# The second feed-forward block's input product: seven half-size products in place of eight from the third tile on

## The chip, the cores and the metric

One core of one Trainium2 chip runs the kernel. The metric is the device time of one execution in microseconds; the time of a version is the median of its runs.

## What is computed

One block of a diffusion transformer, depth 1, on 512 tokens and 256 context tokens of width 1024: a feed-forward block, a mixer (window attention and a gated linear recurrence), and a second feed-forward block. The change concerns the second feed-forward block, which is, for the 512 tokens:

```python
def swiglu(h, w_in, w_out):
    gate, up = jnp.split(h @ w_in, 2, axis=-1)
    return (jax.nn.silu(gate) * up) @ w_out

h = ada_pre(x, norm_pre[l, 2], m[6], m[7])        # rmsnorm, scale, shift
x = ada_post(x, swiglu(h, ffn2_w_in[l], ffn2_w_out[l]), norm_post[l, 2], m[8], 0.5)
```

`w_in` is 1024 x 5632 (gate columns first, then up columns), `w_out` is 2816 x 1024, all in float32.

## The kernel before

Every float32 matrix product runs as three matmuls on operands that were split into a high part (rounded to the engine's short float32 form) and a low residue: `split` makes them with a cast on ScalarE (L65) and a subtraction on VectorE (L66), and `mm3` issues high x high, high x low and low x high (L71, L72, L74) into one PSUM accumulation.

The second feed-forward block keeps the hidden activations transposed, as high and low tiles "hh" and "hl" of 128 partitions x 8 k x tokens. `make_hT` makes them two 128-token groups at a time: for each k two transposes into PSUM (L248), scale and shift (L253 or L255), a cast and a subtraction on VectorE (L257, L258). Its second half is for tokens 256 to 511, which come last from the output projection of the mixer (`y_step`).

`ffn` then walks over 22 tiles, each one 128-column piece of the gate and the same piece of the up weights. For a tile, `in_w` loads a weight piece of 1024 x 128 ("wraw", 512 KB, three buffers) and splits it into "wh" and "wl" (three buffers each); `proj` multiplies it by all 512 tokens: 8 k x 3 matmuls of 512 columns for the gate and the same for up. Then a Silu on ScalarE (L333), the product on VectorE (L335) and a split give "acth" and "actl". The first three weight pieces (both of tile 0, the gate of tile 1) are loaded and split early (`pre2`) and are multiplied in two groups of 256 tokens (`proj_all`), so that TensorE can begin on the first tokens while the last ones are still being made.

Tiles are taken in pieces of 1, 3, 3, 3, 3, 3, 2, 4 (`PIECES`). After the first tile of a piece, `out_phase` multiplies the previous piece's activations by their output weights (`out_w`, buffer "w4" for the raw load, "woh" and "wol" split): for each of four token groups two 512-column halves, added to "yacc" or "tok" (L363, L365). In time, therefore, three input tiles alternate with the output stretch of three tiles.

`mod_gate(2, ...)` makes the gate vector of the last norm from 4 MB of `w_ada`: 16 loads ("wa", two buffers), 16 multiply-adds on VectorE into "macc" (L496, L498), two pairs of matmuls with ones (L507, L508). It stands in the list `background`, and `tick` issues from that list; at the block's first tick all of it is issued, since credit is left over from the first feed-forward block.

The order on each engine's queue is not written by hand here: the framework places instructions by program order as priority, by when it reckons that operands and buffers are ready. All loads are issued on SyncE's queue (SP). [...]

## Time and profile before

| | |
|---|---|
| median of 3 runs | 1497.29 us (1496.05 to 1497.7) |
| the profiled execution | 1498.88 us, its span 1497.1 us |
| mean granted clock of TensorE | 0.991 of full speed |
| busy share of the span | TensorE 97%, VectorE 58%, ScalarE 34% |
| second feed-forward block | from about 1119 us to the end |

Times in rows are microseconds from the span's start. "PE" is TensorE's matmuls, "PEld" its weight loads, "DVE" VectorE, "ACT" ScalarE, "POOL" GpSimd, "SP" the load queue. A duration in a row may overlap the next instruction's, so the distance from one start to the next is the time that an instruction takes of a busy engine.

### The profile page before, as it was taken

What the parts mean: (1) busy time and instruction counts of PE and PEld (TensorE: products, weight loads), DVE (VectorE), ACT (ScalarE), POOL (GpSimd) and SP (SyncE); (2) the same over time, 40 slices, a digit from 0 to 9 for tenths busy, and PEclk for the clock granted to TensorE, in tenths of its full rate; (3) what the DMA queues carried; (4) which work ended last, traced back from release to release, by engine and by line L of the source; (5) the groups of instructions that cost most, each with busy time, mean ns of one, the idle gap of its engine ahead of it and who ended that gap; (6) DMA issues with size and microseconds to landing.
All of it is one profiled execution on the core that took longest, in us unless ns stands there. A gap on an engine that the chain in (4) does not pass through costs nothing.

```text
span 1497.1 us, 20626 instructions
## 1 busy us (share of the span) xinstructions
PE 1445.2 (97%) x8320; PEld 1204.6 (80%) x8320; DVE 870.3 (58%) x1431; ACT 515.9 (34%) x835; POOL 58.3 (4%) x87
## 2 busy tenths in 40 slices
PE   6899999999999999999999899999999999999997
PEld 3688888888788888788889777788778788888886
DVE  6866664675655333857488579843457544433444
ACT  6532121222121222543234468742246222222221
POOL 3200000000000000200001100000010000000001
PEclk9999999999999999999999989999999999999999
DMA  8564332454542111222112211133226533333301
GB/s 305 174 198 128 113 113 69 119 165 141 175 149 71 57 33 53 86 76 61 30 58 60 61 56 43 29 99 99 99 85 207 173 99 99 91 93 106 94 26 56
DMA packets 177895, 151.45 MB, mean 101 GB/s; under 512 B 6408, under 2 KB 152328, under 8 KB 177800
## 3 DMA queue, kind: packets, MB, share of 16 engines
q1 hardware_dynamic: 177800, 150.14, 32.8%
q8 instruction: 65, 1.06, 0.3%
q14 instruction: 30, 0.25, 0.0%
HBM read 148.02 MB, written 2.10 MB: 100 GB/s over the span
## 4 chain that ended last, share of the span: by engine, by line
PE 71%; issue 15%; DVE 6%; ACT 3%; DMA 2%; POOL 2%; SPq 0%; DVEq 0%; POOLq 0%; ACTq 0%
PE mm L71 22%; PE mm L72 22%; PE mm L74 22%; DMA wa<-w_ada 1%; POOL rs L227 1%; PE aux L929 1%; DVE wl L66 1%; DVE wa0l L178 1%; ACT w L224 1%; POOL ss L226 1%; ACT wh L65 0%; PE aux L935 0%; PE aux L507 0%; PE aux L936 0%; DMA tok<-ctx 0%
## 5 line engine op out<-in xcount | busy, mean ns | idle before, releaser
L71 PE MATMUL mm<-hh,wh 128*128 128x512 f32 (+1 forms) x1440 | 513.0, 356 | 0.5 <-ACT sg L333 0.2
L72 PE MATMUL mm<-hl,wh 128*128 128x512 f32 (+1 forms) x1440 | 491.8, 355 | 0.0
L74 PE MATMUL mm<-hh,wl 128*128 128x512 f32 (+1 forms) x1440 | 449.0, 357 | 0.3 <-DVE wl L66 0.3
L71 PEld LDWEIGHTS mm<-hh,wh 128*128 128x128 f32 x1440 | 271.3, 188 | 58.7 <-ACT gg L794 0.7
L72 PEld LDWEIGHTS mm<-hl,wh 128*128 128x128 f32 x1440 | 271.3, 188 | 39.8 <-DVE hl L426 0.6
L65 ACT CAST wh<-wraw 128x1024 fp32r<-128x1024 f32 (+1 forms) x139 | 142.4, 1026 | 461.1 <-PE mm L72 299.9
L66 DVE TENSOR_TENSOR wl<-wraw,wh 128x1024 fp32r<-128x1024 f32 (+1 forms) x139 | 165.5, 1192 | 222.1 <-ACT wh L65 218.9
L74 PEld LDWEIGHTS mm<-hh,wl 128*128 128x128 f32 x1440 | 244.3, 189 | 21.3 <-DVE wl L66 0.5
L71 PE MATMUL mm<-woh,acth 128*128 128x512 f32 x420 | 164.5, 392 | 2.4 <-DVE am L335 2.2
L72 PE MATMUL mm<-wol,acth 128*128 128x512 f32 x420 | 164.1, 391 | 0.0
L498 DVE SCALAR_TENSOR_TENSOR macc<-wa,cs,macc 128x512 f32<-128x512 f32 x140 | 101.8, 750 | 63.3 <-DMA wa<-w_ada 62.6
L74 PE MATMUL mm<-woh,actl 128*128 128x512 f32 x420 | 130.7, 390 | 0.0
L335 DVE TENSOR_TENSOR am<-sg,mm 128x512 f32<-128x512 f32 x66 | 37.5, 595 | 116.0 <-PE mm L74 115.9
L65 ACT CAST woh<-w 128x1024 fp32r<-128x1024 f32 x42 | 44.3, 1055 | 167.9 <-PE mm L74 163.7
L71 PEld LDWEIGHTS mm<-woh,acth 128*128 128x128 f32 x420 | 78.8, 188 | 20.9 <-DVE am L335 3.1
L74 PEld LDWEIGHTS mm<-woh,actl 128*128 128x128 f32 x420 | 78.8, 188 | 16.6
L72 PEld LDWEIGHTS mm<-wol,acth 128*128 128x128 f32 x420 | 78.9, 188 | 15.8
L365 DVE TENSOR_TENSOR tok<-tok,mm 128x512 f32<-128x512 f32 x96 | 61.6, 683 | 51.6 <-PE mm L74 51.6
L66 DVE TENSOR_TENSOR wol<-w,woh 128x1024 fp32r<-128x1024 f32 x42 | 51.2, 1223 | 15.7 <-ACT woh L65 14.4
L226 POOL TENSOR_SCALAR ss<-ss 128x1 f32<-128x1 f32 x30 | 10.4, 345 | 973.2 <-ACT am L224 550.0
L65 ACT CAST acth<-am 128x512 fp32r<-128x512 f32 x66 | 34.1, 549 | 23.4 <-DVE am L335 23.2
L66 DVE TENSOR_TENSOR actl<-am,acth 128x512 fp32r<-128x512 f32 x66 | 37.5, 597 | 0.7 <-ACT acth L65 0.7
(286 smaller groups left out, 1698.6 us busy)
## 6 DMA issues: line engine op xcount, KB each, us to landing
wraw<-ffn_w_in SPq DMA_DIRECT2D x88, 512.0 KB, 4.1
wa<-w_ada SPq DMA_DIRECT2D x128, 256.0 KB, 3.1
w<-ffn_w_out SPq DMA_DIRECT2D x44, 512.0 KB, 4.3
wraw<-mix_w_in SPq DMA_DIRECT2D x42, 512.0 KB, 3.7
tok<-w_ada SPq DMA_DIRECT2D x16, 256.0 KB, 5.6
wraw<-w_out SPq DMA_DIRECT2D x8, 512.0 KB, 4.2
tok<-x SPq DMA_DIRECT2D x4, 512.0 KB, 7.8
wraw<-x SPq DMA_DIRECT2D x4, 512.0 KB, 3.2
```

Source lines behind the costliest of these rows:

```text
L65: nc.scalar.copy(hi, src)
L66: nc.vector.tensor_tensor(out=lo, in0=src, in1=f32(hi), op=ALU.subtract)
L71: nc.tensor.matmul(o, lhsT=sh, rhs=mh, start=start, stop=False)
L72: nc.tensor.matmul(o, lhsT=sh, rhs=ml, start=False, stop=False)
L74: nc.tensor.matmul(o, lhsT=sl, rhs=mh, start=False, stop=stop)
L178: eng.tensor_tensor(out=wl, in0=w, in1=f32(wh), op=ALU.subtract)
L224: nc.scalar.activation(scratch, z, AF.Square, accum_out=ss)
L226: nc.gpsimd.tensor_scalar(ss, ss, 1.0 / n, EPS, ALU.mult, ALU.add)
L227: nc.gpsimd.tensor_tensor(out=r, in0=ss, in1=mhalf, op=ALU.pow)
L335: nc.vector.tensor_tensor(out=m[:, :b - a], in0=s[:, :b - a], in1=up, op=ALU.mult)
L365: nc.vector.tensor_tensor(out=y, in0=y, in1=o[h], op=ALU.add)
L498: nc.vector.scalar_tensor_tensor(out=a, in0=w, scalar=cs[:, v, k:k + 1], in1=a, op0=ALU.mult, op1=ALU.add)
```

## The change

The 2 x 2 x 2 block product (gate and up weights; lower and upper half of k; first and second 256 tokens) is done with seven block products in place of eight, by Winograd's form of Strassen's method, for tiles 2 to 21. Each block product is 4 k x 3 matmuls of 256 columns (`product`). The sums of weight blocks are made for every tile by four VectorE additions of 128x512 (`weights`), with three 1024-wide splits and a 512-wide one in place of two 1024-wide ones. Block sums of the activations (four of them, `sums2`, `sums2_t4`) are made once and kept split beside the blocks themselves, seven forms in all, in the tiles "hh" and "hl". The seven products run through three PSUM accumulators A, B and C; intermediate values are read out of A and C by copies on ScalarE and additions on VectorE before later products are added on top of them. Tiles 0 and 1 are done in the ordinary way, in halves of 256 tokens (`std_tile`).

Around it: `hT_forms` replaces `make_hT` (the cast of two chunks at a time on ScalarE); "w4" moves to a pool of its own ("bx") and holds the unsplit activation blocks too, until the sums are made; `mod_gate` enters the background list after tile 1; the attention's "ov" has one buffer instead of two; the second two token groups are normalised in place; `out_w` and `out_phase` move unchanged into `run_pieces`.

```diff
--- before.py
+++ after.py
@@ -305,7 +305,6 @@
 
         gmax = max(b - a for a, b in groups)
         early = []
-        order = order or range(ntok)
 
         def in_w(j, u):
             return split_w(load_w(w_in[:, u * FF + j * P:u * FF + (j + 1) * P]))
@@ -336,8 +335,13 @@
                 split(ah[:, a:b], al[:, a:b], m[:, :b - a])
             return ah, al
 
+        run_pieces(in_tile, w_out, ntok, pool, pieces, yacc, last, final_pre, order)
+    def run_pieces(in_tile, w_out, ntok, pool, pieces, yacc, last, final_pre=None, order=None, w4=None):
+        order = order or range(ntok)
         def out_w(j):
-            raw = ct([P, D], "w4", bufs=3 if ntok == NX else 4, pool=pool)
+            raw = ct([P, D], "w4", bufs=4, pool=w4 or pool)
             nc.sync.dma_start(raw, w_out[j * P:(j + 1) * P, :])
             if j == NF - 1:
                 hi, lo = ct([P, D], "wh", F32R, bufs=3), ct([P, D], "wl", F32R, bufs=3)
@@ -379,6 +383,117 @@
         if final_pre:
             final_pre()
         out_phase(*prev)
+    F_B11, F_B21, F_B22, F_U1, F_U2, F_T3, F_T4 = range(7)
+    H4 = KD // 2
+    def ffn7(w_in, w_out, forms, nt, ntok, pool, w4, pieces, yacc, last, pre, sums, nstd=2, ticks=0):
+        fh, fl = forms
+        def weights(j):
+            U = load_w(w_in[:, FF + j * P:FF + (j + 1) * P])
+            G = load_w(w_in[:, j * P:(j + 1) * P])
+            A11, A12, A21 = U[:, :H4, :], U[:, H4:, :], G[:, :H4, :]
+            g0 = split_w(U)
+            c = ct([P, H4, P], "wc", pool=pool)
+            ch, cl = ct([P, H4, P], "wch", F32R, pool=pool), ct([P, H4, P], "wcl", F32R, pool=pool)
+            nc.vector.tensor_tensor(out=c, in0=A11, in1=A21, op=ALU.add)
+            nc.vector.tensor_tensor(out=A21, in0=A21, in1=G[:, H4:, :], op=ALU.add)
+            nc.vector.tensor_tensor(out=A11, in0=A11, in1=A21, op=ALU.add)
+            nc.vector.tensor_tensor(out=A12, in0=A12, in1=A11, op=ALU.add)
+            g2 = split_w(U)
+            g1 = split_w(G)
+            split(ch, cl, c)
+            return g0, g1, g2, (ch, cl)
+        def product(o, w, k0, f, first=False):
+            wh, wl = w
+            for k in range(H4):
+                wk, mh, ml = wh[:, k0 + k, :], fh[:, f, k, :], fl[:, f, k, :]
+                nc.tensor.matmul(o, lhsT=wk, rhs=mh, start=first and k == 0, stop=False, skip_group_check=True)
+                nc.tensor.matmul(o, lhsT=wk, rhs=ml, start=False, stop=False, skip_group_check=True)
+                nc.tensor.matmul(o, lhsT=wl[:, k0 + k, :], rhs=mh, start=False, stop=k == H4 - 1,
+                                 skip_group_check=True)
+        def std_half(o, w, half):
+            o = o[:, half * nt:(half + 1) * nt]
+            for k in range(KD):
+                f = ((F_B11, F_B21), (F_T4, F_B22))[half][k // H4]
+                mm3([(o, fh[:, f, k % H4, :], fl[:, f, k % H4, :])], w[0][:, k, :], w[1][:, k, :], k == 0, k == KD - 1)
+        early = []
+        def act(up):
+            ah = ct([P, ntok * P], "acth", F32R, bufs=4, pool=pool)
+            al = ct([P, ntok * P], "actl", F32R, bufs=4, pool=pool)
+            split(ah, al, up.rearrange("p a b -> p (a b)"))
+            return ah, al
+        def std_tile(j):
+            if j == 0:
+                early.extend(ps() for _ in pre)
+                for half in range(2):
+                    for o, w in zip(early, pre):
+                        std_half(o, w, half)
+            gu = []
+            for u in range(2):
+                if early:
+                    o = early.pop(0)
+                else:
+                    w = split_w(load_w(w_in[:, u * FF + j * P:u * FF + (j + 1) * P]))
+                    o = ps()
+                    for half in range(2):
+                        std_half(o, w, half)
+                gu.append(o)
+            up = ct([P, 2, nt], "up", bufs=2, pool=pool)
+            sg = ct([P, 2, nt], "sg", bufs=2, pool=pool)
+            nc.scalar.activation(sg.rearrange("p a b -> p (a b)"), gu[0], AF.Silu)
+            nc.vector.tensor_tensor(out=up.rearrange("p a b -> p (a b)"), in0=sg.rearrange("p a b -> p (a b)"),
+                                    in1=gu[1], op=ALU.mult)
+            return act(up)
+        def in_tile(j):
+            if j < nstd:
+                r = std_tile(j)
+                if j == 0:
+                    sums[0]()
+                if j == nstd - 1:
+                    sums[1]()
+                return r
+            tick(ticks)
+            g0, g1, g2, gc = weights(j)
+            A, B = ps()[:, :nt], ps("aux")[:, :nt]
+            up = ct([P, 2, nt], "up", bufs=2, pool=pool)
+            product(A, g0, 0, F_B11, True)
+            nc.scalar.copy(up[:, 0, :], A)
+            product(B, g0, H4, F_B21, True)
+            nc.vector.tensor_tensor(out=up[:, 0, :], in0=up[:, 0, :], in1=B, op=ALU.add)
+            tick(ticks)
+            C = ps("aux")[:, :nt]
+            sg = ct([P, 2, nt], "sg", bufs=2, pool=pool)
+            product(A, g2, 0, F_U2)
+            nc.scalar.copy(up[:, 1, :], A)
+            product(C, g1, 0, F_U1, True)
+            nc.scalar.copy(sg[:, 1, :], C)
+            product(A, gc, 0, F_T3)
+            nc.vector.tensor_tensor(out=sg[:, 1, :], in0=sg[:, 1, :], in1=A, op=ALU.add)
+            product(C, g2, H4, F_B22)
+            nc.vector.tensor_tensor(out=up[:, 1, :], in0=up[:, 1, :], in1=C, op=ALU.add)
+            nc.scalar.activation(sg[:, 1, :], sg[:, 1, :], AF.Silu, scale=-1.0)
+            product(A, g1, H4, F_T4)
+            nc.scalar.activation(sg[:, 0, :], A, AF.Silu, scale=-1.0)
+            nc.vector.tensor_tensor(out=up, in0=sg, in1=up, op=ALU.mult)
+            return act(up)
+        run_pieces(in_tile, w_out, ntok, pool, pieces, yacc, last, w4=w4)
 
     W = i["mix_w_in"][0]
 
@@ -935,7 +1050,7 @@
                 nc.tensor.matmul(oo[:, cc], lhsT=vk, rhs=th[:, cc], start=u == 0, stop=False)
                 nc.tensor.matmul(oo[:, cc], lhsT=vk, rhs=tl[:, cc], start=False, stop=u == len(kts) - 1)
 
-            ov = ct([P, T], "ov", bufs=2, pool=ma)
+            ov = ct([P, T], "ov", pool=ma)
             nc.scalar.copy(ov[H[0], :], oo[H[1], :])
             nc.vector.tensor_tensor(out=ov[rr, :], in0=oo[H[0], :], in1=ov[H[0], :], op=ALU.add)
             split(oah[rr, g, :], oal[rr, g, :], ov[rr, :])
@@ -963,6 +1078,7 @@
         head_out(*prev)
 
 
+    bx = ctx.enter_context(tc.tile_pool(name="bx", bufs=1, reuse_waits="tile"))
     with tc.tile_pool(name="mg", bufs=1, reuse_waits="tile") as mg:
         merged = {}
 
@@ -989,7 +1105,7 @@
 
         for n in range(KD):
             if n not in sigs:
-                sigs[n] = ct([P, 2 * T], "w4", bufs=4, pool=mg)
+                sigs[n] = ct([P, 2 * T], "w4", bufs=4, pool=bx)
             for u in range(2):
                 if (n, u) in early_gates:
                     g = sigs[n][:, u * T:(u + 1) * T]
@@ -1013,8 +1129,22 @@
                 wout.append((hi, lo))
             pre2 = [split_w(load_w(w2[:, 0:P])), split_w(load_w(w2[:, FF:FF + P])),
                     split_w(load_w(w2[:, P:2 * P]))]
-            hh3 = ct([P, KD, TA], "hh", F32R)
-            hl3 = ct([P, KD, TA], "hl", F32R)
+            N2 = T // 2
+            forms2 = [ct([P, 7, H4, N2], tag, F32R) for tag in ("hh", "hl")]
+            B = {f: ct([P, H4, N2], "w4", bufs=4, pool=bx) for f in (F_B11, F_B21, F_T4, F_B22)}
+            def hT_forms(half, xns):
+                for f, k0 in ((F_B11, 0), (F_B21, H4)) if half == 0 else ((F_T4, 0), (F_B22, H4)):
+                    for k in range(H4):
+                        pt = ps("aux")
+                        for q, xn in enumerate(xns):
+                            nc.tensor.transpose(pt[:, q * P:(q + 1) * P], xn[:, (k0 + k) * P:(k0 + k + 1) * P], ident)
+                        ca, cb = mcol[2, 0](k0 + k)
+                        nc.scalar.activation(B[f][:, k, :], pt[:, :N2], AF.Identity, bias=cb, scale=ca)
+                        if k % 2:
+                            split(forms2[0][:, f, k - 1:k + 1, :], forms2[1][:, f, k - 1:k + 1, :], B[f][:, k - 1:k + 1, :])
             po = [[ps("aux" if t < 2 else "mm") for _ in range(2)] for t in range(NX)]
 
             def y_step(t, k):
@@ -1036,20 +1166,43 @@
                     hc = slice(h * 512, (h + 1) * 512)
                     nc.vector.tensor_tensor(out=z[:, hc], in0=po[t][h], in1=gg[1, 0][:, hc], op=ALU.mult)
                 nc.vector.scalar_tensor_tensor(out=tok[t], in0=z, scalar=r, in1=tok[t], op0=ALU.mult, op1=ALU.add)
-                xns.append(pre_xn(t, ct([P, D], "w4", bufs=4, pool=mg)))
+                xns.append(pre_xn(t, ct([P, D], "xn", bufs=2, pool=mg) if t < 2 else z))
                 if t % 2:
-                    steps([make_hT(2, hh3, hl3, (t - 1, t), xns[-2:], mg)], 1000)
+                    hT_forms(t // 2, xns[-2:])
     mixp.close()
 
 
     with tc.tile_pool(name="f2", bufs=1, reuse_waits="tile") as f2:
-        background.append(mod_gate(2, (0,), 0.5, f2))
+        t4 = []
+        def to_forms(f, k, z):
+            split(forms2[0][:, f, k:k + 2, :], forms2[1][:, f, k:k + 2, :], z)
+        def sums2():
+            for k in range(0, H4, 2):
+                b11, b21, b12, b22 = (B[f][:, k:k + 2, :] for f in (F_B11, F_B21, F_T4, F_B22))
+                U1, U2 = (ct([P, 2, N2], "macc", bufs=2, pool=f2) for _ in range(2))
+                T3, T4 = (ct([P, 2, N2], tag, bufs=2, pool=f2) for tag in ("mx", "wa"))
+                nc.vector.tensor_tensor(out=U1, in0=b11, in1=b12, op=ALU.subtract)
+                nc.vector.scalar_tensor_tensor(out=U2, in0=U1, scalar=-1.0, in1=b22, op0=ALU.mult, op1=ALU.subtract)
+                to_forms(F_U2, k, U2)
+                to_forms(F_U1, k, U1)
+                nc.vector.tensor_tensor(out=T3, in0=b22, in1=b12, op=ALU.subtract)
+                to_forms(F_T3, k, T3)
+                nc.vector.scalar_tensor_tensor(out=T4, in0=U2, scalar=-1.0, in1=b21, op0=ALU.mult, op1=ALU.subtract)
+                t4.append(T4)
+        def sums2_t4():
+            for k in range(0, H4, 2):
+                to_forms(F_T4, k, t4[k // 2])
+            background.append(mod_gate(2, (0,), 0.5, f2))
         yacc = [ct([P, D], "tok", bufs=6) for _ in range(2)] + [ct([P, D], "yacc", bufs=2, pool=f2) for _ in range(2)]
 
         def last2(t, o):
             y = yacc[t]
             s2 = ct([P, 2], "ss2", bufs=4)
-            yg = ct([P, D], "w4", bufs=3, pool=f2)
+            yg = ct([P, D], "w4", bufs=4, pool=bx)
             junk = ct([P, 512], "junk", pool=f2)
             hs = [slice(h * 512, (h + 1) * 512) for h in range(2)]
             for h, hc in enumerate(hs):
@@ -1066,8 +1219,8 @@
                                                op0=ALU.mult, op1=ALU.add)
                 nc.sync.dma_start(out[0, t * P:(t + 1) * P, hc], y[:, hc])
 
-        ffn(i["ffn2_w_in"][0], i["ffn2_w_out"][0], (hh3, hl3), ((0, T),), NX, f2, PIECES, yacc, last2,
-            groups0=((0, 256), (256, T)), pre=pre2, ticks=1)
+        ffn7(i["ffn2_w_in"][0], i["ffn2_w_out"][0], forms2, N2, NX, f2, bx, PIECES, yacc, last2,
+             pre=pre2, sums=(sums2, sums2_t4), ticks=1)
 
 
 _INS = ["x", "c", "ctx", "c_ctx", "w_ada", "b_ada", "norm_pre", "norm_post", "ffn1_w_in", "ffn1_w_out",
```

## Rows read from the trace of the kernel before

**Rows 1.** The page: busy time by engine, and the chain that ended last.
```profile
PE 1445.2 (97%) x8320; PEld 1204.6 (80%) x8320; DVE 870.3 (58%) x1431; ACT 515.9 (34%) x835; POOL 58.3 (4%) x87
...
PE 71%; issue 15%; DVE 6%; ACT 3%; DMA 2%; POOL 2%; SPq 0%; DVEq 0%; POOLq 0%; ACTq 0%
```

**Rows 2.** Windows: an input stretch of three tiles and the output stretch behind it.
```profile
core 0: us, PE busy (x) PEld busy (x) DVE busy (x) ACT busy (x) POOL busy (x), PEclk, DMA share, GB/s
...
1205.80:1238.46 32.66, 32.66 (x146) 27.03 (x145) 12.20 (x13) 8.89 (x11) 0.00 (x0) 1.00 0.43 128
1238.46:1254.80 16.34, 16.34 (x73) 13.52 (x72) 7.65 (x11) 3.71 (x4) 0.00 (x0) 1.00 0.12 34
```

**Rows 3.** Waits of DVE, 1190 to 1400 us: total, times, longest.
```profile
DVE am L335 <- PE mm L74: 43.9, 13, 3.4
```

**Rows 4.** Timeline of DVE in the same stretch: start, duration.
```profile
1217.80 1.23 DVE L66 TENSOR_TENSOR wl<-wraw,wh 128x1024 fp32r<-128x1024 f32 x1
...
1228.68 1.23 DVE L66 TENSOR_TENSOR wl<-wraw,wh 128x1024 fp32r<-128x1024 f32 x1
...
1239.56 1.23 DVE L66 TENSOR_TENSOR wl<-wraw,wh 128x1024 fp32r<-128x1024 f32 x1
...
1250.71 1.28 DVE L365 TENSOR_TENSOR yacc<-yacc,mm 128x512 f32<-128x512 f32 x2 [2.79 <-PE mm L74]
```

**Rows 5.** Timeline of PE: its waits in the block's start.
```profile
1127.33 0.66 PE L248 MATMUL aux<-ident,w 128*128 128x128 f32 x4 [0.66 <-DVE w L232]
...
1157.86 0.50 PE L507 MATMUL aux<-mx,ones 128*128 128x512 f32 x1 [1.48 <-ACT mx L65]
...
1178.17 0.50 PE L507 MATMUL aux<-mx,ones 128*128 128x512 f32 x1 [2.28 <-ACT mx L65]
```

**Rows 6.** Timeline of PE: first and last of 81 matmuls of 256 columns in tile 0.
```profile
1130.67 0.28 PE L71 MATMUL mm<-hh,wh 128*128 128x256 f32 x1
...
1140.27 0.28 PE L74 MATMUL mm<-hh,wl 128*128 128x256 f32 x1
```

**Rows 7.** Timeline of PE's weight loads there.
```profile
1139.07 0.19 PEld L74 LDWEIGHTS mm<-hh,wl 128*128 128x128 f32 x1
1139.19 0.19 PEld L71 LDWEIGHTS mm<-hh,wh 128*128 128x128 f32 x1
```

**Rows 8.** Timeline of ACT, 1129 to 1141 us.
```profile
1129.20 1.02 ACT L255 ACTIVATE h<-aux,colB,colA 128x256 f32<-128x256 f32 x2 [0.77 <-DVE hl L258]
...
1138.50 0.62 ACT L65 CAST acth<-am 128x512 fp32r<-128x512 f32 x1
1139.03 1.04 ACT L65 CAST wh<-wraw 128x1024 fp32r<-128x1024 f32 x1
1139.98 1.05 ACT L65 CAST woh<-w 128x1024 fp32r<-128x1024 f32 x1
```

**Rows 9.** Timeline of DVE, 1127 to 1143 us.
```profile
1127.69 0.54 DVE L253 TENSOR_SCALAR h<-aux,colA,colB 128x256 f32<-128x256 f32 x1 [0.42 <-PE aux L248]
...
1133.73 0.43 DVE L258 TENSOR_TENSOR hl<-h,hh 128x256 fp32r<-128x256 f32 x1
...
1139.92 0.68 DVE L66 TENSOR_TENSOR actl<-am,acth 128x512 fp32r<-128x512 f32 x1
1140.52 0.75 DVE L498 SCALAR_TENSOR_TENSOR macc<-wa,cs,macc 128x512 f32<-128x512 f32 x1
1141.18 1.22 DVE L66 TENSOR_TENSOR wl<-wraw,wh 128x1024 fp32r<-128x1024 f32 x1
1142.31 1.22 DVE L66 TENSOR_TENSOR wol<-w,woh 128x1024 fp32r<-128x1024 f32 x1
```

**Rows 10.** Waits of SP's queue from 1119 us on.
```profile
SPq L341 <- DVE w L232: 28.2, 1, 28.2
```

**Rows 11.** The page: loads, KB each, median us from issue to landing.
```profile
wa<-w_ada SPq DMA_DIRECT2D x128, 256.0 KB, 3.1
w<-ffn_w_out SPq DMA_DIRECT2D x44, 512.0 KB, 4.3
```

**Rows 12.** Line L498 from 1119 us on: count, durations in ns, first and last start.
```profile
L498 DVE SCALAR_TENSOR_TENSOR macc<-wa,cs,macc x14: 744/752/754, 1140.5 to 1176.7; 128x512 f32<-128x512 f32 x14
```

**Rows 13.** Timeline of DVE: first, second and last two of eight writers of "ov".
```profile
882.19 0.68 DVE L940 TENSOR_TENSOR ov<-aux,ov 64x512 f32<-64x512 f32 x1
903.39 0.68 DVE L940 TENSOR_TENSOR ov<-aux,ov 64x512 f32<-64x512 f32 x1
...
966.38 0.68 DVE L940 TENSOR_TENSOR ov<-aux,ov 64x512 f32<-64x512 f32 x1 [0.18 <-ACT ov L939]
973.52 0.68 DVE L940 TENSOR_TENSOR ov<-aux,ov 64x512 f32<-64x512 f32 x1 [1.20 <-ACT ov L939]
```

## Prediction

> **What bounds the kernel now.** I read the page first: TensorE (PE) is busy 97% of the span, VectorE (DVE) 58%, ScalarE (ACT) 34%, and the chain that ended last is 71% PE [rows 1]. The change lies in the last quarter, from 1119 us on, so I read that stretch alone by windows. It repeats with a period of three tiles (a tile is one 128-column pair of gate and up): an input stretch of 32.66 us and an output stretch of 16.34 us. In both PE is busy for the whole window at granted clock 1.00, and DVE is busy 12.20 and 7.65 us of them [rows 2]. The waits confirm the direction: DVE waits for PE, 43.9 us in that part for the activation product alone [rows 3]. So what sets the end here is the start-to-start distance of matmuls, and one input tile lasts as long as the same DVE split recurs: 1228.68 − 1217.80 = 10.88 us, and 10.88 again [rows 4]. A tile is 48 matmuls of 512 columns (2 weights x 8 k x 3), so 10.88 / 48 = 226.7 ns each.
>
> The exception is the start of the stage. While the hidden activations and the gate vector of the last norm are made, PE waits for both: 0.66 us once for a transpose, and 1.48 and 2.28 us for the gate's matmuls [rows 5].
>
> **The seven-product tile on PE.** A half-size product is 12 matmuls (4 k x 3) of 256 columns; seven are 84. Their price is in this trace, since tile 0 already runs in halves: from 1130.67 to 1140.27 there are 80 steps at 9.60 us, or 120.0 ns [rows 6], each with its own weight load of 0.19 us that overlaps its neighbours [rows 7]. So a tile goes from 10.88 to 84 x 0.1200 = 10.08 us: 0.80 us less, not the eighth (1.36 us) that the count of columns promises. The two prices give (226.7 − 120.0) / 256 = 0.417 ns a column and 13.3 ns fixed a matmul; 36 more matmuls pay 0.48 us of that fixed part. Twenty tiles: **−16.0 us**.
>
> [...]
>
> Tile 1's up column is now done in halves too: 48 x 0.1200 − 24 x 0.2267 = **+0.3 us**. Tile 0 was in halves already; nothing.
>
> **What DVE and ACT get per seven-product tile.** Prices are start-to-start distances of neighbours [rows 8, 9]: on DVE a 1024-wide split residue 1.13 us (1141.18 to 1142.31), a 512-wide operation 0.60 (1139.92 to 1140.52), with a scalar 0.66; on ACT a 1024-wide cast 0.95 (1139.03 to 1139.98), a 512-wide 0.53. A 256-wide read from PSUM is not there as an add or copy; nearest are DVE's 0.54 us (tensor_scalar) and ACT's two in 1.02, so 0.51 [rows 8, 9]. From below, half of the 512-wide prices (0.30 and 0.27) bounds them; I take 0.42, midway, for DVE and 0.51 for ACT.
> DVE: three splits 3.39, the sum's split 0.60, four weight sums 2.40, three adds from PSUM 1.26, product and activation split 1.20: 8.85 us in 10.08. ACT: three casts 2.85, two small ones 1.06, three copies and two Silus 2.55: 6.5 us.
> Over three tiles and their output stretch: PE 3 x 10.08 + 16.34 = 46.6 us; DVE 3 x 8.85 + 3 x 1.13 (output weights) + 8 x 0.64 (output sums, two in 1.28 [rows 4]) = 35.1 us, 75%, against 19.9 of 49.0 before. So DVE is nearly twice as busy but not the bound, provided its work can be done ahead.
>
> Can it? Within a tile, counted from its first matmul, the products start every 1.44 us. The first operand set g0 is free after product 2 (2.88), so the next tile's g0 is split by 5.3. The weight sums follow to 6.5. g2 is free after product 6 (8.64): cast to 9.7, residue to 11.0; the next tile needs it at 10.08 + 2.88 = 12.96. g1 is free at 10.08: cast to 11.6 behind the Silu, residue to 12.8; needed at 14.40. Both have 1.6 to 2 us to spare, one DVE operation of 1.13 us and not two. Reading the accumulators between products has 1.44 us less the evacuation of 0.5, also enough behind at most one other operation. The cover is therefore thin; where the copies of output weights (three pairs of 0.95 and 1.13) fall into it, PE waits some tenths. For the 17 tiles from 5 on I take 0.1 us each, **+1.7 us**; bounds nothing and 0.8 a tile (13.6).
>
> **The start of the stage.** (a) The activations: the old path made each of eight chunks by a transpose, ACT or DVE, a DVE cast and a DVE residue; the second half ran from 1127.33 to 1134.16 [rows 5, 9]. The new one moves casts to ACT in pairs of chunks: per pair 2 x 0.51 + 0.53 on ACT and then 0.60 on DVE, four pairs 6.2 + 0.6 us and semaphores, about the same end, but a pair is released later than a single chunk. PE had these chunks just in time. **+1 us**, bounds 0 and 4.
> (b) The sums over activations: 8 sums and 6 residues on DVE before the third tile, 8 x 0.63 + 6 x 0.60 = 8.6 us, and 1.2 for the last form after tile 1. They lie under tile 0's end (6 us), tile 1's up column (5.8) and the first output stretch (24 matmuls, 5.6). The first output weight now waits for a buffer that holds one of the operands, until the second pair's first sum, four sums and two residues (3.8 us) after the activations, at about 1138.5; in the trace SP's queue stood before this load too, 28.2 us in one wait [rows 10]. It lands 4.3 us later (the median of these loads [rows 11]), is split by 1145, and is wanted at about 1147. Queued behind it on SP: the weights of tile 3, wanted at about 1160, and the gate's loads. Nothing, with 2 us to spare.
> (c) The gate of the last norm: 14 multiply-adds in 1140.5 to 1176.7 [rows 12], paced by their loads (3.1 us each [rows 11], two buffers). It now starts after tile 1, so at about 1150, and falls on tiles 2 to 4, where DVE is fullest. DVE from 1134.7 to the end of tile 4: sums 9.8, weights of tiles 2 to 4 19.2, their evacuations 4.9, two old activations 2.4, tile 1's weight 1.1, four output weights 4.5, gate 14.7 (16 x 0.66, 6 x 0.69): 56.6 us, where PE needs 6 + 5.8 + 5.6 + 30.2 + 0.9 = 48.5. The excess is 8 us if all had to be ready; but the gate isn't wanted before the end of the kernel and its loads spread it over some 36 us. **+3 us**, bounds 0 and 8. The 3.8 us that PE waits for the gate's matmuls today [rows 5] I leave: they are issued the same way. If they vanish it is −3.8.
>
> **The rest, at nothing.** The single "ov" buffer: its writers are 7 to 21 us apart [rows 13], and the split that frees it follows within some 2 us; were that cover gone, each head would wait those 2 us. The "w4" pool moved out: same four buffers. The second pair of tokens normalised in place: same operations. The last output stretch: the last activation comes by the same four steps, after 4 us of matmuls that don't need it.
>
> **Sum.** −16.0 + 0.3 + 1 + 3 + 1.7 = −10.0 us. The profiled execution took 1498.88 us (span 1497.1 and 1.8 around it), 0.1% over the median of 1497.29; so the changed kernel's profile should be near 1489 and its median **1487.3 us**.
>
> **Rivals.**
> 1. *The vector engines eat it.* DVE's order of instructions is fixed beforehand, so an evacuation that waits for PE stops the weight work behind it. If PE loses 0.4 to 0.7 us per tile, half to all of the 0.80 is gone: 1492 to 1498. For it: 8.85 of 10.08 us in a tile. Against it: 75% over the period, and the trace shows DVE waiting for PE, not the reverse [rows 3].
> 2. *Slower.* The same place, one step further: g1 is free only at the tile's end and reaches product 4 at 4.32 us; cast, residue and what the fixed order puts ahead (two output residues, 2.3 us, or three) make 2.2 + 2.3 to 3.4 = 4.5 to 5.6. It decides where the waits pass 16 us in all: 0.8 us a tile, or 0.6 with the 4.3 us of the start. At 1.3 us a tile, 20 x 0.5 + 4.3 = 14 us slower: about 1511. Should the start cost its upper bounds (4 + 8), 0.2 a tile is enough. [...]
> 3. *More.* No waits in the tiles, and the later start of the gate frees PE of its 3.8 us: −16 − 3.8 + 1 = near 1479; with part of it, 1483.
> 4. *The fixed cost of a matmul is not paid in the products*: the columns alone save (48 x 512 − 84 x 256) x 0.417 ns = 1.28 us a tile, 25.6 in all, so 1478 with the other terms. The mean over all 80 steps, 120.0 ns, speaks against it. [...]
>
> **Chances.** Forecast, a gain of 5 to 15 us (1482 to 1492): 0.60. Rival 1: 0.16, half of it within the noise. Rival 2: 0.15. Rival 3: 0.07. Rival 4: 0.02. About 0.2%, 3 us, is what a measurement of this kernel tells from no change. Faster 0.60 + 0.08 + 0.09 = 0.77, same 0.08, slower 0.15. The likeliest case's own range is 1482 to 1492; the range given goes up to rival 1's end and the mildest of rival 2, and down to rival 3: 1480 to 1499, which leaves out most of rival 2 and part of 3 and 4, under 0.2.
>
> **What would show it.** In the profile after: products at 120 ns and 84 of them in 10.1 to 10.3 us in the tiles from 5 on; the three-tile period 46.6 to 47.2 us; DVE near 75% there. A period over 49.0 means rival 2, and then PE's waits name a weight residue ("wl") or DVE's add into "sg". In the start, the end of tile 4 relative to the end of tile 0 says whether the sums and the gate cost 3 us. Wrong altogether would be a 256-column pace other than 120 ns, or losses outside the stage (attention, buffer "ov").

## The result, and the profile after

The changed kernel takes **1510.2 us** (median of 4 runs, 1509.52 to 1511.06) against 1497.49 (1496.05 to 1499.49, 4 runs) for the kernel before: ratio 1.0084, 95% interval 1.0067 to 1.0102. It is slower by 12.7 us. Forecast were 1487.3 us, and slower with a chance of 0.15 only.

The page of the changed kernel, the lines that answer to [rows 1], with the clock's line:

```profile
PE 1433.2 (95%) x9064; PEld 1228.2 (81%) x9064; DVE 984.5 (65%) x1601; ACT 583.2 (39%) x973; POOL 59.2 (4%) x87
...
PEclk9999999999999999999999999999999799999999
...
PE 68%; issue 15%; DVE 7%; DMA 4%; ACT 3%; POOL 2%; SPq 0%; DVEq 0%; POOLq 0%; ACTq 0%
```

PE has 12 us less work than before and yet the span is 12 us longer, so PE waits. DMA has twice its share of the chain that ended last (4% for 2%): loads are on it. And it is in one place: one of 40 slices has a granted clock below the rest. The windows of that place, with one input stretch of three tiles and its output stretch from later on (the two that answer to [rows 2]); columns as there:

```profile
1152.00:1158.00 6.00, 3.64 (x26) 2.98 (x24) 5.74 (x8) 4.46 (x7) 0.00 (x0) 1.00 0.85 256
1158.00:1170.00 12.00, 1.68 (x12) 1.48 (x12) 6.87 (x10) 1.35 (x3) 0.00 (x0) 0.79 0.78 244
1170.00:1186.00 16.00, 1.69 (x3) 0.74 (x3) 7.89 (x12) 0.71 (x2) 0.00 (x0) 0.50 0.49 149
1186.00:1190.00 4.00, 4.00 (x16) 3.46 (x17) 0.51 (x1) 0.26 (x1) 0.00 (x0) 0.50 0.47 120
1190.00:1194.00 4.00, 4.00 (x25) 3.81 (x25) 3.70 (x6) 1.58 (x3) 0.00 (x0) 0.72 0.03 11
1194.00:1198.00 4.00, 4.00 (x35) 4.00 (x35) 2.21 (x4) 2.27 (x4) 0.00 (x0) 1.00 0.02 4
...
1232.16:1262.31 30.15, 30.15 (x253) 30.14 (x252) 26.22 (x38) 17.47 (x28) 0.00 (x0) 1.00 0.41 123
1262.31:1278.68 16.37, 16.37 (x75) 13.52 (x73) 10.10 (x14) 4.06 (x5) 0.00 (x0) 1.00 0.22 65
```

The later stretch is what the change was to bring: 252 matmuls of 256 columns in 30.15 us, 119.6 ns each (120.0 in [rows 6]), 10.05 us a tile (10.88 in [rows 4]), PE busy all the time, DVE 36.3 us of 46.5 (78%). Between 1158 and 1186 PE is busy for 3.4 us of 28, and neither DVE nor ACT is full. Who waits there: the waits of PE in the whole block, and the timeline of PE in that stretch (this answers to [rows 5]):

```profile
PE aux L622 <- ACT mx L65: 24.4, 2, 14.2
PE mm L421 <- ACT up L476: 2.0, 1, 2.0
...
PE mm L421 <- ACT up L483: 0.5, 1, 0.5
```

```profile
1153.40 0.28 PE L423 MATMUL mm<-hh,wl 128*128 128x256 f32 x1
1155.70 0.39 PE L421 MATMUL mm<-hh,wh 128*128 128x256 f32 x1 [2.02 <-ACT up L476]
...
1158.26 0.38 PE L421 MATMUL mm<-hh,wch 128*128 128x256 f32 x1 [0.46 <-ACT up L483]
...
1159.66 0.28 PE L423 MATMUL mm<-hh,wcl 128*128 128x256 f32 x1
1170.14 0.79 PE L622 MATMUL aux<-mx,ones 128*128 128x512 f32 x1 [10.21 <-ACT mx L65]
...
1185.83 0.80 PE L622 MATMUL aux<-mx,ones 128*128 128x512 f32 x1 [14.17 <-ACT mx L65]
1186.56 0.80 PE L623 MATMUL aux<-mx,ones 128*128 128x512 f32 x1
1187.15 0.41 PE L421 MATMUL aux<-hh,wh 128*128 128x256 f32 x1
```

L622 is the gate's matmul with ones (L507 before). `ps` makes the accumulators, by the kernel's text four buffers, called banks here, under the tag "mm" and four under "aux". Read the order of the products in tile 2: the first, third and fifth, all into accumulator A ("mm"), run one behind the other until 1159.66. The second product comes first in the program's text after the first, but it goes into B, which is "aux", and it runs only at 1187.15, behind both of the gate's pairs, which are "aux" too. Before the change PE waited for the same two matmuls for 1.48 and 2.28 us [rows 5]; products on "mm" filled the rest of the time.

The gate itself is only a little later than it was. Its multiply-adds (this answers to [rows 12]) start 12.8 us later and end 7.6 us later:

```profile
L613 DVE SCALAR_TENSOR_TENSOR macc<-wa,cs,macc x14: 747/751/754, 1153.3 to 1184.3; 128x512 f32<-128x512 f32 x14
```

**Where the 12.2 us between the two spans lie** (1509.3 − 1497.1). Tiles 2 to 4 took 63.7 us (1152.09 to 1215.80), before 38.0 (1151.45 to 1189.44): +25.7. The 17 tiles from 5 on: 10.05 for 10.89 us each, −14.2. From the block's first product to tile 2: 33.8 against 31.9 us, +2.0; the block began 1.3 us earlier. Sum +12.2. Of the 33.5 us by which tiles 2 to 4 exceed 3 x 10.05, 26.9 are the waits above, 2.9 the gate's four matmuls (1170.14 to 1171.67 and 1185.83 to 1187.15), and 2.2 the low clock behind the wait: the 24 matmuls of tile 2's second and fourth product take 5.1 us (1187.15 to 1192.26), and at 0.1196 us each they would take 2.9. The other 1.5 were not followed.

### The profile page after: what moved, and what is told of

Read it like the earlier page. It is cut to its first block, busy times and chain, and to the rows that moved or that the text cites. A ratio compares the mean times of both kernels' runs of the same rounds, so it can differ in the third digit from the quotient of the medians.

```text
span 1509.3 us, 22491 instructions
## 1 busy us (share of the span) xinstructions
PE 1433.2 (95%) x9064; PEld 1228.2 (81%) x9064; DVE 984.5 (65%) x1601; ACT 583.2 (39%) x973; POOL 59.2 (4%) x87
## 4 chain that ended last, share of the span: by engine, by line
PE 68%; issue 15%; DVE 7%; DMA 4%; ACT 3%; POOL 2%; SPq 0%; DVEq 0%; POOLq 0%; ACTq 0%
PE mm L71 17%; PE mm L74 16%; PE mm L72 16%; DMA wa<-w_ada 3%; PE mm L421 2%; PE mm L422 2%; PE mm L423 2%; PE aux L421 2%; PE aux L422 2%; PE aux L423 2%; DVE macc L613 1%; POOL rs L227 1%; DVE wl L66 1%; PE aux L1044 1%; POOL ss L226 1%
## 5 line engine op out<-in xcount | busy, mean ns | idle before, releaser
L71 PE MATMUL mm<-hh,wh 128*128 128x512 f32 (+1 forms) x1128 | 388.9, 346 | 0.5 <-ACT sg L332 0.2
L72 PE MATMUL mm<-hl,wh 128*128 128x512 f32 (+1 forms) x1128 | 368.0, 343 | 0.0
L74 PE MATMUL mm<-hh,wl 128*128 128x512 f32 (+1 forms) x1128 | 325.5, 346 | 0.7 <-DVE wl L66 0.7
L71 PEld LDWEIGHTS mm<-hh,wh 128*128 128x128 f32 x1128 | 212.1, 188 | 46.0 <-ACT gg L909 0.7
L72 PEld LDWEIGHTS mm<-hl,wh 128*128 128x128 f32 x1128 | 212.4, 188 | 27.2 <-DVE hl L541 0.8
L421 PE MATMUL mm<-hh,wh 128*128 128x256 f32 x240 | 68.1, 284 | 2.0 <-ACT up L476 2.0
L421 PE MATMUL aux<-hh,wh 128*128 128x256 f32 x240 | 69.1, 288 | 0.0
L422 PE MATMUL aux<-hl,wh 128*128 128x256 f32 x240 | 69.0, 287 | 0.0
L423 PE MATMUL aux<-hh,wl 128*128 128x256 f32 x240 | 68.9, 287 | 0.0
L423 PE MATMUL mm<-hh,wl 128*128 128x256 f32 x240 | 67.8, 283 | 0.1
```

The source lines that it names most:

```text
L71: nc.tensor.matmul(o, lhsT=sh, rhs=mh, start=start, stop=False)
L72: nc.tensor.matmul(o, lhsT=sh, rhs=ml, start=False, stop=False)
L74: nc.tensor.matmul(o, lhsT=sl, rhs=mh, start=False, stop=stop)
L421: nc.tensor.matmul(o, lhsT=wk, rhs=mh, start=first and k == 0, stop=False, skip_group_check=True)
L422: nc.tensor.matmul(o, lhsT=wk, rhs=ml, start=False, stop=False, skip_group_check=True)
L423: nc.tensor.matmul(o, lhsT=wl[:, k0 + k, :], rhs=mh, start=False, stop=k == H4 - 1, skip_group_check=True)
```

## The experiments

Theory A: PSUM accumulators of one tag are given out in the order in which the program first writes them, so the gate, issued whole at tile 2's first tick, stands ahead of tile 2's B and C on PE, and their products wait behind it. Theory B: the gate is simply late, because its loads and multiply-adds begin after tile 1 and DVE is fuller; any kernel with so late a gate waits. Theory C, from the prediction: the sums and splits on DVE delay the products. Diffs are against the changed kernel unless said otherwise; version 1 is the kernel of experiment 1, and so on. The kernel before, run beside them, had medians of 1495.75 to 1497.78 us. The runs of one version spread over 1 to 4 us, so a version with one run can be read to some 2 us. The profiles of the versions show the block's first product between 1114.9 (version 6) and 1120.4 us (version 8), though no experiment changes anything ahead of it: where two profiles are compared, that much is not the block's. In the diffs "..." stands for lines left out.

**1. Other tags for the accumulators.** All banks of A, B and C under "mm", the output stretch's under "aux".

```diff
-                o = [ps() for _ in range(2)]
+                o = [ps("aux" if w4 else "mm") for _ in range(2)]
...
-            A, B = ps()[:, :nt], ps("aux")[:, :nt]
+            A, B = ps()[:, :nt], ps()[:, :nt]
...
-            C = ps("aux")[:, :nt]
+            C = ps()[:, :nt]
```

> The changed kernel with the PSUM tags exchanged in the second block: the accumulators A, B and C all under "mm", the two banks of each output step under "aux". The gate's matmuls stay under "aux" and start after tile 1 as before. Theory A (banks of one tag are handed out in program order, so the products into B and C of tile 2, which share "aux" with the gate, stand behind the gate's two pairs of matmuls, and those wait for 4 MB of loads): TensorE fills the time with products, its wait for the gate falls from 24.4 us to 5 to 10, and the time to 1490 to 1496 us. Theory B (the gate comes late, and TensorE has to wait for its loads wherever its matmuls stand): a wait of 20 us or more, 1506 to 1511 us. Theory C (VectorE is overloaded in tiles 2 to 4 and holds TensorE up): waits for the weight residue or the evacuations take the gate's place, 1503 us or more.

1490.91 us (5 runs; ratio 0.996, 0.9946 to 0.9974). The wait for the gate falls from 24.4 to 2.9 us, though the gate is as late (its pairs begin at 1167.65 and 1187.96, in the changed kernel at 1170.14 and 1185.83): PE does products meanwhile. Other waits came up (weights, 4.9 us):

```profile
PE mm L421 <- ACT wh L65: 4.9, 4, 3.6
PE aux L622 <- ACT mx L65: 2.9, 1, 2.9
```

**2. No gate.** The gate vector is a constant 0.5, so its 4 MB of loads, its sums and matmuls are left out.

```diff
-            background.append(mod_gate(2, (0,), 0.5, f2))
+            gg[2, 0] = ct([P, D], "gg", bufs=3)
+            nc.vector.memset(gg[2, 0], 0.5)
```

> The changed kernel without the gate of the last norm: its 16 loads, 16 multiply-adds, casts, residues and matmuls are left out, and the gate vector is a constant (so the last norm's scaling is left out of the computation). Theories A and B: all of the gate's cost goes, tiles 2 to 4 take 30.2 to 32 us in place of 63.7, and the time is 1478 to 1483 us. Theory C without the gate's 14.7 us of VectorE: tiles 2 to 4 still show waits for weight residues of 3 us or more, 1483 to 1490 us.

1475.94 us (1 run), a little below what was expected. Tiles 2 to 4 take 30.39 us, and the list of PE's waits from 1100 us to the end is this:

```profile
PE aux L1142 <- DVE tok L232: 1.4, 2, 0.8
PE aux L1142 <- DVE xn L232: 0.8, 2, 0.6
PE mm L74 <- DVE wl L66: 0.4, 1, 0.4
```

All lie ahead of tile 2, the last at 1139.32, in tile 1's up product. The sums over activations and weights delay no product: theory C has nothing left for tiles 2 to 4.

**3. The gate in steps.** The credit left over is dropped, so the gate's steps enter the program two a tile.

```diff
             background.append(mod_gate(2, (0,), 0.5, f2))
+            credit[0] = 0.0
```

> The changed kernel with one line more: the credit of the background list is set to zero when the gate enters it, so that each tick issues one of its steps (two a tile) and not all at once in tile 2. The first pair of gate matmuls then stands after tile 5, the second after tile 9. Theory A: their operands are there when their turn in the order of banks comes, TensorE waits under 1 us for them in all, 1480 to 1485 us. Theory B: what is waited for is the loads, so with the matmuls still later than they are now there is nothing to win by spreading them unless the waits shrink with the distance; 1490 us or more. Theory C: VectorE has the gate's work spread thin, so this can't be told from theory A here.

1485.79 us (4 runs; ratio 0.9926, 0.9911 to 0.9941). No wait for the gate is left, though its loads begin at 1148 as in the changed kernel: only its place in the order is another. But 9.9 us remain against no gate, and 1485.79 lies just above the range expected; PE's waits name the weights and DVE's add:

```profile
PE mm L421 <- DVE sg L487: 3.0, 3, 1.5
PE mm L421 <- ACT wh L65: 2.0, 1, 2.0
```

**4. The kernel before, with the gate from tile 4 on.** The list gets the gate at tile 4 of eight products.

```diff
+            if j == 4 and late:
+                background.append(late[0]())
...
-        background.append(mod_gate(2, (0,), 0.5, f2))
```

> The kernel before, with nothing changed but that the gate enters the background list at tile 4 and not at the start of the block, so its loads and matmuls come some 17 us or more later, as they do in the changed kernel. Nothing else uses the banks of "aux" there. Theory A: lateness alone costs nothing; TensorE waits 0 to 6 us for the gate (3.8 in the kernel before), 1494 to 1500 us. Theory B: lateness is the cause, a wait of 20 us, about 1515 us.

1498.22 us (1 run), one wait of 3.6 us. Against B, but weakly: the loads began at 1139.1, 8 us later than before and still 9 earlier than in the changed kernel, since no operand held them. Experiment 9 repeats it with an operand that does.

**5. The ticks at the end of a tile.** The gate still enters all at once, but behind tile 2's products.

```diff
-            tick(ticks)
...
-            tick(ticks)
...
-            return act(up)
+            r = act(up)
+            tick(2 * ticks)
+            return r
```

> The changed kernel with both ticks moved to the end of a seven-product tile, so that the whole of tile 2 stands ahead of the gate in program order, and tile 3 behind it. Theory A (order of banks): TensorE can do tile 2 and then three products of tile 3 before it stands at the gate: 120 matmuls in place of 36 before the wait, which ends when the gate's loads end, as before. The wait falls by about 84 x 0.12 = 10 us, from 24.4 to some 14, and the time from 1510 to about 1500 us. Theory B (TensorE waits for the late gate wherever it stands): the loads too start a tile later, and the wait stays at 20 us or more, 1506 to 1511 us.

1501.87 us (1 run), a wait of 13.5 us for the gate and 4.2 for weights: one tile's work more goes ahead of the gate, and the wait shortens by about that.

```profile
PE aux L622 <- ACT mx L65: 13.5, 1, 13.5
```

**6. The gate's banks under "mm".**

```diff
-                o = ps("aux")
+                o = ps(tag)
...
-            background.append(mod_gate(2, (0,), 0.5, f2))
+            background.append(mod_gate(2, (0,), 0.5, f2, "mm"))
```

> The changed kernel with the second block's gate moved from the PSUM tag "aux" to "mm", nothing else. Theory A: the tag decides which products stand behind the gate. Now those into A (under "mm") do, and the three into B and C (under "aux") go ahead: again 36 matmuls before the wait, so the wait keeps its size, 22 to 27 us, and the time is 1507 to 1513 us; the trace shows products into "aux" ahead of the gate and none into "mm". If it is not the tag but something that only B's and C's products need (a form, a weight sum), the products into A go ahead as they do now, and the wait hardly changes either, but the order does.

1507.99 us (1 run). The mirror image: now the gate's matmuls hold up A, and the products into "aux" go ahead of them.

```profile
PE mm L622 <- ACT mx L65: 23.9, 2, 14.6
```

```profile
1156.51 0.28 PE L423 MATMUL aux<-hh,wl 128*128 128x256 f32 x1
1166.10 0.80 PE L622 MATMUL mm<-mx,ones 128*128 128x512 f32 x1 [9.32 <-ACT mx L65]
...
1182.22 0.80 PE L622 MATMUL mm<-mx,ones 128*128 128x512 f32 x1 [14.60 <-ACT mx L65]
...
1183.54 0.42 PE L421 MATMUL mm<-hh,wh 128*128 128x256 f32 x1
```

**7. The gate's ticks in the output stretches.**

```diff
+                if w4 and not final:
+                    tick(0.75)
...
+            credit[0] = 0.0
...
-             pre=pre2, sums=(sums2, sums2_t4), ticks=1)
+             pre=pre2, sums=(sums2, sums2_t4), ticks=0)
```

> The changed kernel with the gate issued in the output stretches: no ticks in the tiles, credit set to zero when the gate enters the list, and in each output stretch but the last three of its steps (three quarters of a tick for each of four token groups). If the 10 us by which the paced gate (1485.8) stays above the kernel without a gate (1475.9) come from its multiply-adds standing in VectorE's queue, and its loads in SP's, among the work of a tile, they go, since in the output stretches VectorE has little to do: 1477 to 1480 us, and no wait for "sg" or "wh" over 0.5 us in the tiles from 2 on. If they come from the volume of the loads or the gate's own matmuls, they stay: 1484 to 1487 us.

1484.83 us (4 runs; ratio 0.9914, 0.9897 to 0.993): missed. The gate was meant to move into the output stretches, but the loads still began at 1147.0 and the multiply-adds at 1150.9: the ticks gave the gate another rank and not another time, since no operand held it back. PE waits 2.8 us for a weight at 1167.6.

**8. More work on DVE, no gate.** Version 2 with four more 128x512 additions a tile, results unused.

```diff
+            for _ in range(4):
+                nc.vector.tensor_tensor(out=ct([P, H4, P], "junk", pool=pool), in0=U[:, :H4, :], in1=U[:, H4:, :],
+                                        op=ALU.add)
```

> The kernel without the gate (it leaves the last norm's gate out, as before), with four additions of 128x512 more on VectorE in every seven-product tile, ahead of the second weight split; their result is not used. That is 2.4 us of VectorE a tile, two operations of the size that the prediction called one too many. If the cover is as thin as the prediction had it (room for one operation of 1.13 us ahead of a weight residue and not for two), TensorE waits 0.3 to 1 us in each tile: 1482 to 1496 us. If there is more room, the tiles stay at 10.05 us and the time at 1475 to 1478 us.

1483.02 us (1 run). By the time alone that is the range expected of a thin cover, but the tiles say otherwise: from tile 8 on three tiles take 30.20 to 30.23 us, some 0.02 a tile over version 2's 30.15, with DVE busy 28.9 us of them. DVE has room for four additions, 2.4 us in all at the 0.60 us of [rows 9], in each tile, where the prediction had given it room for one operation of 1.13 us and not for two. Of the 7 us over version 2, 3.8 lie ahead of the block's first product (1120.44 for 1116.61), where nothing was changed, and 1.7 in three waits in tiles 3 and 7; the rest wasn't followed.

**9. The kernel before with a gate that can't start early.** Its multiply-adds read a copy of their scalars that is made from tile 2's activation (against the kernel before).

```diff
+            if gate_at and j == 2:
+                gate_at(ah)
...
-                        nc.vector.scalar_tensor_tensor(out=a, in0=w, scalar=cs[:, v, k:k + 1], in1=a,
+                        nc.vector.scalar_tensor_tensor(out=a, in0=w, scalar=csv[0][:, v, k:k + 1], in1=a,
...
+        def start_gate(ah):
+            late = ct([P, 2, KD], "late", pool=f2)
+            nc.vector.scalar_tensor_tensor(out=late[:, 0, :], in0=f32(ah[:, :KD]), scalar=0.0, in1=cs[:, 0, :],
+                                           op0=ALU.mult, op1=ALU.add)
+            csv[0] = late
+            background.append(mod_gate(2, (0,), 0.5, f2))
```

> The kernel before, with eight products in every tile, but the gate's multiply-adds can't start before tile 2's activation (the same dependency), which is later than in the changed kernel; all is issued at once as before. If being late is what makes TensorE wait, it waits some 20 us for the gate's matmuls here too: about 1515. If the wait comes from accumulators of the same kind standing behind the gate's, which in this kernel only the gate has, TensorE goes on with the products of the other kind: a wait of 0 to 6 us, 1494 to 1500.

1494.1 us (1 run). The timeline of PE at the gate's two pairs:

```profile
1178.34 0.50 PE L510 MATMUL aux<-mx,ones 128*128 128x512 f32 x1 [1.57 <-ACT mx L65]
...
1196.33 0.51 PE L510 MATMUL aux<-mx,ones 128*128 128x512 f32 x1 [1.75 <-ACT mx L65]
```

They are 8.2 and 10.5 us later than in the changed kernel, and PE waits 3.3 us instead of 24.4. Theory B falls here.

**10. The gate late and in steps.** As 3, but its multiply-adds wait for tile 6's activation, by the same copy; **11** is the same without the reset of the credit, so that all enters at once in tile 7.

```diff
+            if j == 6:
+                gate_at(r[0])
...
```

> The changed kernel, but the gate of the last norm can start only when tile 6's activation is there (its multiply-adds read a copy of their scalars that is made from it), and it is then issued two steps a tile, so that its two pairs of matmuls fall far behind the loads and sums that they need. If what is left in the paced version is the crowd at the start (the gate's loads and multiply-adds in tiles 2 to 4 beside the first weight sums), it goes away: nearly no wait but the first normalisation's, 1477 to 1480. If the gate's work itself is the cost wherever it lies (4 MB of loads, 16 operations on VectorE, four long matmuls), the time stays at 1484 or more.

> As the late, paced gate, but all of the gate's steps are issued at once in tile 7, away from the start of the block, where nothing else is late. If the order of the accumulators' first use is the cause, the seven-product tile that follows has its second and third accumulator behind the gate's matmuls: TensorE does the products into the first one and the output stretch, then waits 10 to 25 us for the gate: about 1490 to 1500. If the cause was the crowd at the start of the block, nothing is left of it here: 1478 to 1481.

Version 11: 1495.15 us (1 run). Far from the block's start, where nothing else is late, one of the gate's pairs stops PE again, and the products into "aux" stand behind it:

```profile
1253.79 0.79 PE L626 MATMUL aux<-mx,ones 128*128 128x512 f32 x1 [14.62 <-ACT mx L65]
1254.52 0.79 PE L627 MATMUL aux<-mx,ones 128*128 128x512 f32 x1
1255.11 0.41 PE L422 MATMUL aux<-hh,wh 128*128 128x256 f32 x1
```

Version 10: 1485.84 us (4 runs; ratio 0.993, 0.9913 to 0.9947), the same as version 3 and no 1477 to 1480: the crowd at the start was not what is left there. Tiles 2 to 4 now take 30.15 us, and the waits have gone with the gate, to tiles 8 and 9. The window of the largest:

```profile
1248.00:1256.00 8.00, 4.68 (x27) 4.07 (x26) 8.00 (x12) 3.76 (x5) 0.00 (x0) 0.84 0.63 191
```

DVE is busy for all of the 8 us, and PE for 4.68. The steps entered two a tile, but the multiply-adds ran in a bunch, 14 of them from 1223.2 to 1256.9.

**12. One step a tile.** One of the gate's 16 multiply-adds can start with each tile from 2 on, held by that tile's activation; the other ticks are off.

```diff
+            gate_at(j, r[0])
...
+        def gate_step(j, ah):
+            late = ct([P, 2, KD], "late", bufs=2, pool=f2)
...
+            csv[0] = late
+            if j == 2:
+                background.append(mod_gate(2, (0,), 0.5, f2))
+            tick(1)
```

> The changed kernel, with one of the gate's 16 loads and multiply-adds a tile: from tile 2 on each multiply-add reads a copy of its scalars that is made from that tile's activation, so it can't start earlier, and the gate's two pairs of matmuls come behind tiles 10 and 18, with their sums long made. If what is left in the paced versions (about 10 us over the version without a gate, 1475.94) comes from the gate's operations falling on two or three tiles at once, where VectorE has no room for them, it goes away: no wait in the tiles, 1475 to 1479. If each of the gate's operations costs wherever it lies, the time stays at 1483 or more.

**1477.98 us** (4 runs, 1476.48 to 1479.06, against 1497.42 in 7; ratio 0.9871, 0.9855 to 0.9888), with the whole gate in it, and 2 us over the version without one. The windows of a stretch that holds one of the gate's steps a tile, the multiply-adds, and PE's waits from 1100 us to the end:

```profile
1289.74:1320.30 30.56, 30.56 (x255) 30.39 (x253) 27.23 (x41) 16.09 (x27) 0.00 (x0) 1.00 0.46 139
1320.30:1336.44 16.14, 16.14 (x74) 13.33 (x73) 10.90 (x17) 4.91 (x6) 0.00 (x0) 1.00 0.27 82
```

```profile
L616 DVE SCALAR_TENSOR_TENSOR macc<-wa,late,macc x14: 744/744/749, 1173.8 to 1399.7; 128x512 f32<-128x512 f32 x14
```

```profile
PE aux L1145 <- DVE tok L232: 1.3, 2, 0.8
PE aux L1145 <- DVE xn L232: 0.8, 2, 0.6
PE mm L74 <- DVE wl L66: 0.4, 1, 0.4
```

The same 16 operations that cost some 10 us in versions 3 and 10 cost about 2 when they are spread over 16 tiles. From the block's first product to the end, versions 2, 3, 10 and 12 take 357.5, 367.9, 368.3 and 359.5 us in their profiles, so the differences are the block's; but version 2 has one run, and 2 us are hardly told from nothing. This version beats both kernels.

## Why the prediction was wrong

**The tile's price** held. Forecast 10.08 us for 84 matmuls, measured 10.05 (119.6 for 120.0 ns). Rival 4 falls with it: it needed 10.88 − 1.28 = 9.60 us a tile. The 13.3 ns fixed a matmul stay the prediction's estimate, from [rows 4] and [rows 6].

**The waits in the tiles**, +0.1 us each with bounds of nothing and 0.8, were mis-sized: the 17 tiles from 5 on have none worth a tenth. Rivals 1 and 2 both lean on this thin cover. DVE's share was right (75% forecast, 78% measured); that only one operation of 1.13 us more has room was wrong, by version 8, at least for operations whose operands are there. Slower did come, as rival 2 said, but by another mechanism: rival 2's own sign, a three-tile period over 49.0 us, is not there (30.15 + 16.37 = 46.5), and the waits name the gate and no weight residue in these tiles. That its 1511 us lie near the measured 1510.2 is chance. What rival 1 says of DVE's order is in the trace after, at a small size: the sum L411 has its operands when L410 ends, at 1193.88, and starts at 1194.95, behind an evacuation that waits 0.73 us for PE. No wait of PE came of it.

```profile
1193.20 0.68 DVE L410 TENSOR_TENSOR wraw<-wraw,wraw 128x512 f32<-128x512 f32 x1
1194.62 0.42 DVE L489 TENSOR_TENSOR up<-up,aux 128x256 f32<-128x256 f32 x1 [0.73 <-PE aux L423]
1194.95 0.69 DVE L411 TENSOR_TENSOR wraw<-wraw 128x512 f32<-128x512 f32 x1
```

**The start, (a) and (b).** Tile 1 and the activations were to cost 1.3 us and cost 2.0, the sums nothing, and version 2 confirms that: within their bounds.

**The step that failed is in (c)**: "The 3.8 us that PE waits for the gate's matmuls today [rows 5] I leave: they are issued the same way." They are, but what stands behind them isn't. In tiles 2 to 4 of the kernel before the gate is alone on "aux", and PE does products on "mm" until the gate's operands come (3.8 us of waits, 3.3 in version 9); after the change two of a tile's three accumulators are "aux" as well, and all of the gate is issued ahead of them. I counted what the gate costs DVE and not what it does to PE's order. The +3 us for DVE was mis-sized too. Its list of DVE's work has the price of two tiles' evacuations for three (4.9 = 2 x 2.46; three are 7.4), and the trace shows DVE busy for 60.0 us from 1134.7 to the end of tile 4, not 56.6. And version 3, where the order is mended, is 10 us over no gate, version 12 is 2. The terms for tiles 2 to 4 were −2.4 and +3; measured: +25.7.

What is shown: taking the gate out (2), from the front (5), into steps (3), or the accumulators to another tag (1) removes between 45% and all of the wait; swapping the tags swaps which products stand (6); a later gate alone does not make it (9); a gate issued at once does it again elsewhere (11). That the framework orders by first use is read from PE's timeline in these versions; how it decides is not shown. A rival is left that no run tests by itself, a lack of free banks; by the kernel's text it should not hold tile 2, since the gate takes two of the four "aux" banks and tile 2's B and C the other two. In the 24.4 us no matmul passed the gate's in the changed kernel, with the second product's operands long there (the first product used the same weights' other half, from 1152.09 on): PE kept the order that the framework gave it, which is not that of the program's text (there B's product comes before A's second).

**Rival 3** (no waits in the tiles and the gate's 3.8 us gone, near 1479) is what the change is worth when the gate doesn't stand in its way: version 12 is at 1478.

**Left open**: what exactly makes the gate's steps cost 10 us in versions 3 and 10. Version 10's window shows DVE full and version 12 shows that spreading ends it, but it spreads the loads as well; version 8 shows that a nearly full DVE alone doesn't do it. The multiply-adds also wait for their loads in DVE's queue, 4.0 us in version 10, and ACT stood there for 11.3 us (to 1235.53) at the cast of the gate's first sum; in version 7 it stood 9.2 us at the second (to 1248.4), and the three tiles from 1252.33 took 30.15 us all the same. Part of the 10 us is slower matmuls: in version 10 the granted clock of the 8 us from 1248 was 0.84 (the window above), and in version 3 the matmuls that start from 1169.69 to 1171.18 come 0.213 us apart, 0.7 us more for the seven steps than at 0.12. Which share each of these has was not tried alone.

## What to carry to other kernels

When a change gives new work an accumulator, list what else uses that tag in that stretch and in which order the program first writes them: here the gate's group waited for a slow chain, tile 2's second product stood behind it on the same tag, and PE waited 24.4 us. Where a wait costs little today (3.8 us here), name the work that covers it, and see whether the change takes it away. Spread background work by what its operands wait for: where only its place in the program was moved (version 7), its loads still began at 1147.0 and the time was 1484.83 us; with one step held by an operand of each tile (version 12) it was 1477.98.

## What was not expected of the hardware

PE did 1.7 us of work in the 12 us from 1158 and 1.7 in the 16 us from 1170, and its granted clock was 0.79 and then 0.50 of full speed. It was still 0.50 from 1186 to 1190 with PE busy throughout, 0.72 in the next 4 us and 1.00 only from 1194. Matmuls of 256 columns came 0.21 us apart there (starts at 1187.15, 1187.37, 1187.58) instead of 0.12. So beside the wait itself some 2 us went in the matmuls behind it: 5.1 us for 24 that take 2.9 at the later pace. What sets the clock was not tried.
